# Two-layer hybrid trunk: nine instead of seven feed-forward blocks by a seven-product scheme, with its ordinary units, sums and additions placed anew

## The chip, the core and the metric

The kernel runs on one core of one Trainium2 chip. The metric is device time in microseconds (us) of one execution. In the text PE is TensorE, DVE is VectorE, ACT is ScalarE, POOL is GpSimd and SP is SyncE, which here only issues loads. A "layer" is one of the two layers of the model.

## The reference

Two layers over 256 tokens of width 2048, in float32. The first half of a layer computes `z = RMSNorm(x) @ w_in`, a gated unit on 16 channel groups, windowed attention on 16 heads, and `x += concat(RMSNorm(A), RMSNorm(B)) @ w_out`. The change bears on the second half, the feed-forward part:

```python
h2 = rms_norm(x, norm2_g[l])
x = x + (jax.nn.silu(h2 @ w_gate[l]) * (h2 @ w_up[l])) @ w_down[l]
```

`w_gate` and `w_up` are 2048 x 5632 and `w_down` is 5632 x 2048. The output is x after both layers.

## The kernel before

**Numbers in two halves.** Every weight is split into a high part `wh` (what the fast float32 form of TensorE keeps) and a rest `wl = w - wh`; activations are split likewise, once. A product is three matmuls (`mm3`, lines 124 to 127): high by high, high by low, low by high, each 128 x 128 against 128 x 512. The split of a loaded piece (`split2`, lines 89 to 98) is one cast on ACT (line 95) and one subtraction on DVE (line 96), each over 128 x 1024 elements.

**Units.** A piece is 512 KB of weights: 128 rows by two groups of 512 columns. `raw_load` (line 82) loads it from SP's queue into one of 6 rotating buffers. An ordinary unit (`unit`) loads one piece, splits it and makes 12 matmuls: two groups by two blocks of 128 tokens by three. `wh` and `wl` have 4 buffers each, so the splits can be at most four units ahead of PE. Instructions stand on each engine's queue in an order that the framework's scheduler makes at build time from the order of the program.

**The feed-forward part.** The 5632 columns of `w_gate` and `w_up` are 11 blocks of 512. An ordinary block (`gate_up`) takes 16 units, 8 for the gate and 8 for the up projection: 192 matmuls. A block by products (`seven`) sees rows of the two projections and the two token blocks as a 2 x 2 scheme and computes it by seven products instead of eight, with sums of activations (`ext`, made once in `combine`) and sums of weights: 28 product units of 6 matmuls each, 168 in all. Its first phase keeps four sums in PSUM (tiles `m`), 4 steps of four product units; each step loads three pieces (`b11`, `b12`, `b22`) and DVE makes three sums over 128 x 1024 (lines 594 to 596). The second phase keeps three (tiles `n`), 4 steps of three product units; each step loads two pieces and DVE adds one of them to a kept sum (line 621). Between and behind the phases, at a "turn", DVE and ACT combine the products out of PSUM (lines 605 to 612 and 626 to 632), and `act_T` transposes the finished block on PE and splits it.

**What stands beside the products.** The product units of the seven blocks in `S_BLOCKS` come from `s_stream`; the ordinary units, in the order of `STD_ORDER`, come from `std_stream`: the other four blocks (`gu`) and the down projection (`down`), in groups of one or two finished blocks. For each product unit 0.71 (0.5 x `STD_SHARE`) ordinary units are owed, and at a turn at least two. A `down` group whose blocks aren't finished yet yields nothing. What is left of the ordinary units runs after the last block. The down projection adds each group of output columns from PSUM to the residual `xres` on DVE (line 680). Ordinary units accumulate in the PSUM tiles `dacc`, after the last block in `acc`.

Of the kernel before, what the change touches and what calls it, by code (L numbers as in the profile page):

```python
# [12 lines left out]
F32 = mybir.dt.float32  # L13
F32R = mybir.dt.float32r
BF16 = mybir.dt.bfloat16
# [6 lines left out]
P = 128  # L22
# [4 lines left out]
HD = 64  # L27
# [12 lines left out]
NI = 3584 // NB  # L40
NFF = DFF // NB
ND = D // NB
S_BLOCKS = (1, 3, 5, 7, 8, 9, 10)
STD_ORDER = (
    ("gu", 0), ("gu", 2), ("down", (0, 1)), ("gu", 4), ("down", (2, 3)), ("gu", 6),
    ("down", (4, 5)), ("down", (6, 7)), ("down", (8, 9)), ("down", (10,)),
)
STD_SHARE = 1.42
RL = 512
WARM = 12  # L50

# [12 lines left out]
def trunk(ctx, tc, x, xt, w_in, w_out, w_gate, w_up, w_down, sgu_w, sgu_g, consts,  # L64
# [15 lines left out]
        return t.bitcast(F32)  # L80

    def raw_load(src, parts=1):
        raw = wp.tile([P, 2, NB], F32, tag="raw", name="raw", bufs=6)
        n = 2 // parts
        for i in range(parts):
            nc.sync.dma_start(raw[:, i * n : (i + 1) * n, :], src[:, i * n : (i + 1) * n, :])
        return raw
# [60 lines left out]

    cst = cp.tile([P, L, C_L], F32, tag="cst", name="cst")
    nc.sync.dma_start(cst, consts)  # L150
    junk = cp.tile([P, NB], BF16, tag="junk", name="junk")
    nc.vector.memset(junk, 1.0)
    heat = small_ps([P, NB], "heat")
    for i in range(WARM):
# [8 lines left out]
    def small(shape, name):  # L163
        return sp.tile(shape, F32, tag=name, name=name)
# [27 lines left out]
        return ps  # L192

    def sum_sq(dst, src):
        nc.scalar.activation(junk[:, : src.free_size()], src, AF.Square, accum_out=dst)

    def finish_rms(ss, width):
        tot = small([P, 1], "tot")
# [57 lines left out]
    for lay in range(L):  # L256
# [71 lines left out]
        def attend(g, t, par, zkv=zkv, kT=kT, qT=qT, ob=ob, bias=bias, layer=layer):  # L328
            nk = (t + 1) * P
            k0 = SEQ - nk  # L330
            nh = 2 * len(par)
            heads = [h for h in range(GRP) if h % 2 in par]
            step = heads[1] - heads[0]
            nkb = nk // P
            nsink = layer["nsink"]
            s = ap.tile([P, nh, nk], F32, tag="spt", name="s", bufs=4)
            for r in par:
                ps = small_ps([P, 2, nk], "ps_s")
                for i in range(2):
                    h = g * GRP + 2 * i + r  # L340
                    nc.tensor.matmul(
                        ps[:, i, :],
                        qT[h // 8][HD * r : HD * r + HD, (h % 8) // 2, t * P : (t + 1) * P],
                        kT[HD * r : HD * r + HD, g, :nk],
                        start=True,
                        stop=True,
                    )
                nc.vector.scalar_tensor_tensor(
                    s[:, par.index(r) :: len(par), :], ps, 1.0 / math.sqrt(HD),
                    bias[g][:, r::2, k0:], ALU.mult, ALU.add,  # L350
                )
            m = small([P, nh], f"m{nh}")
            nc.vector.tensor_reduce(m, s, AX.X, ALU.max)
            hs = slice(g * GRP + heads[0], (g + 1) * GRP, step)
            nm = small([P, nh], f"nm{nh}")
            nc.vector.scalar_tensor_tensor(nm, m, -1.0, nsink[:, hs], ALU.mult, ALU.min)
            es = small([P, nh], f"es{nh}")
            nc.vector.tensor_tensor(es, nm, nsink[:, hs], ALU.subtract)
            den = small([P, nh], f"den{nh}")
            for i in range(nh):  # L360
                nc.scalar.activation(
                    s[:, i, :], s[:, i, :], AF.Exp, bias=nm[:, i : i + 1],
                    accum_out=den[:, i : i + 1],
                )
            nc.scalar.activation(es, es, AF.Exp)
            rden = small([P, nh], f"rden{nh}")
            nc.vector.tensor_tensor(rden, den, es, ALU.add)
            nc.vector.reciprocal(rden, rden)
            pt = ap.tile([P, nh * nkb, P], F32, tag="spt", name="pt", bufs=4)

            def turn():
                pst = small_ps([P, nh * nkb, P], "ps_p")
                s4 = s.rearrange("p h (b k) -> p (h b) k", k=P)
                for i in range(nh * nkb):
                    nc.tensor.transpose(pst[:, i, :], s4[:, i, :], ident)
                nc.vector.tensor_copy(pt, pst)

            def weigh():
                pv = small_ps([P, nh, HD], "ps_v")
                for i in range(nh):  # L380
                    for b in range(nkb):
                        nc.tensor.matmul(  # L382
                            pv[:, i, :],
                            pt[:, i * nkb + b, :],
                            zkv[b][:, (NKV + g) * HD : (NKV + g + 1) * HD],
                            start=b == 0,
                            stop=b == nkb - 1,
                        )
                if (g, t) not in ob:
                    ob[g, t] = ap.tile([P, GRP * HD], F32, tag=f"ob{t}", name="ob", bufs=1)  # L390
                o3 = ob[g, t].rearrange("p (h d) -> p h d", d=HD)
                nc.vector.tensor_tensor(o3[:, heads[0] :: step, :], pv, bc(rden, HD), ALU.mult)

            later(3, turn)
            later(5, weigh)
# [172 lines left out]
        def seven(b, lay=lay, pairs2=pairs2, ext2=ext2, act_later=act_later):  # L568
# [9 lines left out]
            def a_op(k, t):  # L578
                return lambda p, h: pairs2[p][:, h, k, t * P : (t + 1) * P]
# [2 lines left out]
                return lambda p, h: ext2[p][:, h, n, :]  # L582

            kept = []
            for i in range(4):
                b12 = raw_load(w_up[lay, b, i, 0])
                b11 = raw_load(w_gate[lay, b, i, 0])
                b22 = raw_load(w_up[lay, b, i, 1])
                t1 = wp.tile([P, 2, NB], F32, tag="raw", name="t1", bufs=6)
                t2 = ap.tile([P, 2, NB], F32, tag="spt", name="t2", bufs=4)  # L590
                first, last = i == 0, i == 3
                s_unit(b11, 0, i, a_op(0, 0), first, last)
                yield 0.5
                nc.vector.tensor_tensor(t1, b11, b12, ALU.add)
                nc.vector.tensor_tensor(t2, t1, b22, ALU.add)
                nc.vector.tensor_tensor(b12, b12, b22, ALU.add)
                s_unit(t1, 1, i, e_op(1), first, last)
                yield 0.5
                s_unit(t2, 3, i, e_op(2), first, last)
                yield 0.5  # L600
                s_unit(b12, 2, i, e_op(0), first, last)
                yield 0.5
                kept.append(t2)
            m1 = zp.tile([P, NB], F32, tag="z", name="m1")
            nc.scalar.copy(m1, bank[0])
# [9 lines left out]
            for i in range(4):  # L615
                b21 = raw_load(w_gate[lay, b, i, 1])
                b22 = raw_load(w_up[lay, b, i, 1])
                first, last = i == 0, i == 3
                s_unit(b21, 0, i, a_op(1, 0), first, last)
                yield 0.5  # L620
                nc.vector.tensor_tensor(kept[i], kept[i], b21, ALU.add)
                s_unit(kept[i], 1, i, a_op(1, 1), first, last)
                yield 0.5
                s_unit(b22, 2, i, e_op(3), first, last)
                yield 0.5
            sg = [m1, c21]
            for t, m in ((0, m1), (1, c21)):
                nc.vector.tensor_tensor(m, bank[t], m, ALU.add)
# [36 lines left out]
        def down(blocks, final, lay=lay, pairs_f=pairs_f, norm_block=norm_block, ss1=ss1, pairs1=pairs1):  # L665
            for n in range(ND):
                while any(len(pairs_f.get(b, [])) < 2 for b in blocks):
                    yield False
                acc = new_acc() if seven_done[0] else new_acc(pd, "dacc")
                for k, b in enumerate(blocks):  # L670
                    for c in range(2):
                        pair = pairs_f[b][c]
                        unit(
                            w_down[lay, b, n, c], [(pair, 0), (pair, 1)], acc,
                            k == 0 and c == 0, k == len(blocks) - 1 and c == 1,
                        )
                        yield True
                for t in range(NTOK):
                    xs = xres[:, t, n * NB : (n + 1) * NB]
                    nc.vector.tensor_tensor(xs, acc[t], xs, ALU.add)  # L680
                    if final and lay == L - 1:
                        nc.sync.dma_start(out[t * P : (t + 1) * P, n * NB : (n + 1) * NB], xs)
                if final and lay < L - 1:
                    norm_block(n, ss1, pairs1, lay + 1, C_G1)
# [8 lines left out]
        other = std_stream()  # L693
        owed = 0.0
        for said in s_stream():
            owed = max(owed, 2.0) if said == "turn" else owed + said * STD_SHARE
            while owed >= 1.0 and next(other, False):
                owed -= 1.0
        seven_done[0] = True
        for went in other:  # L700
            if not went:
# [89 lines left out]
```

## Time and profile before

| | |
|---|---|
| median of three runs | 2026.76 us (2026.12 to 2032.09) |
| the profiled execution | 2025.57 us |
| its span, first to last instruction | 2023.9 us |
| PE busy | 1984.0 us (98%) |
| DVE busy | 1666.0 us (82%) |
| ACT busy | 1132.3 us (56%) |
| POOL busy | 67.5 us (3%) |
| moved by DMA | 416.02 MB, mean 206 GB/s |
| feed-forward part of the first layer, first product to the next layer's first matmul | 299.9 to 1015.6 us |
| of the second layer, to the last matmul | 1305.5 to 2019.3 us |

Busy time of PE is the time covered by records of matmuls, which overlap; the distance from start to start of two matmuls says what one costs. A row of the table by groups has the line, the engine, the operation, output <- inputs, shapes and the count; behind the bar busy time, mean nanoseconds of one, then the engine's idle time just before and what ended it.

### The profile page before, as it was taken

Reading aid. Unit: us, or ns where it says so; the run is one execution under the profiler, and the core shown is the slowest. Engines: PE = TensorE matmul, PEld = TensorE weight load, DVE = VectorE, ACT = ScalarE, POOL = GpSimd, SP = SyncE. Lnnn points to the kernel's source line nnn. Section 1 sums busy time; section 2 is a strip of 40 time slices with the busy share of each in tenths; the row PEclk is TensorE's granted clock in tenths of the full one; section 3 lists DMA queues with packets and bytes.
Section 4 is the critical chain, followed back from the end, with each engine's and each line's share of the span. In section 5 each row is a group of like instructions: output and inputs, shape, how many; then the busy total and the mean of one; then the engine's idle time right before and its main releaser. Section 6 shows DMA issues by size and latency. Waiting matters only on the chain.

```text
span 2023.9 us, 24694 instructions
## 1 busy us (share of the span) xinstructions
PE 1984.0 (98%) x8990; PEld 1618.5 (80%) x8990; DVE 1666.0 (82%) x1925; ACT 1132.3 (56%) x1415; POOL 67.5 (3%) x65
## 2 busy tenths in 40 slices
PE   8999999999999999999899999999999999999997
PEld 6878888888888888877687788888888888888776
DVE  5767689898989898997867776898989898989976
ACT  6455566555555555554654655666555555555543
POOL 1211000000000000000002100000000000000000
PEclk9999999999999999999999999999999999999999
DMA  9643556565766576665555344565656565657653
GB/s 323 226 162 134 187 178 227 201 235 194 238 209 234 201 236 212 234 204 193 198 188 192 131 156 179 175 233 203 239 206 234 202 239 202 233 204 241 215 186 137
DMA packets 117401, 416.02 MB, mean 206 GB/s; under 512 B 12912, under 2 KB 15088, under 8 KB 117280
## 3 DMA queue, kind: packets, MB, share of 16 engines
q1 hardware_dynamic: 115136, 407.01, 58.4%
q0 software_dynamic: 2144, 7.44, 1.2%
q8 instruction: 70, 1.15, 0.2%
q14 instruction: 51, 0.42, 0.1%
HBM read 412.27 MB, written 4.23 MB: 206 GB/s over the span
## 4 chain that ended last, share of the span: by engine, by line
PE 85%; DVE 9%; issue 2%; DMA 1%; ACT 1%; POOL 1%; SPq 0%; POOLq 0%; ACTq 0%; DVEq 0%
PE dacc L125 12%; PE dacc L126 12%; PE dacc L127 12%; PE acc L126 8%; PE acc L125 8%; PE acc L127 8%; DVE wl L96 4%; PE m L126 4%; PE m L127 4%; PE m L125 4%; PE n L126 3%; PE n L127 3%; PE n L125 3%; PE ps_v L382 1%; DMA raw<-in_w_gate_dram 1%
## 5 line engine op out<-in xcount | busy, mean ns | idle before, releaser
L95 ACT CAST wh<-raw 128x1024 fp32r<-128x1024 f32 (+1 forms) x706 | 739.5, 1050 | 593.2 <-PE dacc L127 293.2
L96 DVE TENSOR_TENSOR wl<-raw,wh 128x1024 fp32r<-128x1024 f32 (+1 forms) x706 | 853.7, 1219 | 207.9 <-ACT wh L95 198.5
L95 ACT CAST wh<-t 128x1024 fp32r<-128x1024 f32 x168 | 177.1, 1054 | 184.6 <-PE dacc L127 116.9
L125 PE MATMUL dacc<-wh,aT 128*128 128x512 f32 x640 | 251.4, 393 | 2.3 <-DVE xres L680 1.5
L127 PE MATMUL dacc<-wh,aT 128*128 128x512 f32 x640 | 250.0, 391 | 0.0
L126 PE MATMUL dacc<-wl,aT 128*128 128x512 f32 x640 | 249.9, 391 | 0.0
L96 DVE TENSOR_TENSOR wl<-t,wh 128x1024 fp32r<-128x1024 f32 x168 | 204.0, 1219 | 17.4 <-ACT wh L95 15.4
L125 PE MATMUL dacc<-wh,hT 128*128 128x512 f32 x512 | 200.3, 391 | 0.3
L126 PE MATMUL dacc<-wl,hT 128*128 128x512 f32 x512 | 199.5, 390 | 0.3 <-DVE wl L96 0.2
L127 PE MATMUL dacc<-wh,hT 128*128 128x512 f32 x512 | 199.4, 389 | 0.0
L126 PE MATMUL acc<-wl,hT 128*128 128x512 f32 x448 | 176.8, 395 | 7.8 <-DVE wl L96 7.8
L125 PE MATMUL acc<-wh,hT 128*128 128x512 f32 x448 | 180.6, 406 | 2.1 <-ACT wh L95 2.1
L127 PE MATMUL acc<-wh,hT 128*128 128x512 f32 x448 | 176.6, 394 | 0.0
L125 PEld LDWEIGHTS dacc<-wh,aT 128*128 128x128 f32 x640 | 120.1, 188 | 30.1 <-issue 3.1
L127 PEld LDWEIGHTS dacc<-wh,aT 128*128 128x128 f32 x640 | 120.7, 189 | 25.6
L126 PEld LDWEIGHTS dacc<-wl,aT 128*128 128x128 f32 x640 | 120.9, 189 | 24.5
L126 PE MATMUL m<-wl,ext 128*128 128x512 f32 x336 | 132.6, 395 | 4.6 <-DVE wl L96 4.6
L125 PE MATMUL m<-wh,ext 128*128 128x512 f32 x336 | 132.7, 395 | 1.1 <-ACT wh L95 1.1
L127 PE MATMUL m<-wh,ext 128*128 128x512 f32 x336 | 132.1, 393 | 0.0
L125 PE MATMUL acc<-wh,aT 128*128 128x512 f32 x320 | 127.8, 399 | 0.7 <-ACT aT L560 0.7
L126 PE MATMUL acc<-wl,aT 128*128 128x512 f32 x320 | 125.3, 392 | 0.0
L127 PE MATMUL acc<-wh,aT 128*128 128x512 f32 x320 | 124.1, 391 | 0.0
(157 smaller groups left out, 2980.7 us busy)
## 6 DMA issues: line engine op xcount, KB each, us to landing
raw<-in_w_up_dram SPq DMA_DIRECT2D x232, 512.0 KB, 4.3
raw<-in_w_gate_dram SPq DMA_DIRECT2D x176, 512.0 KB, 4.1
raw<-in_w_down_dram SPq DMA_DIRECT2D x176, 512.0 KB, 4.1
raw<-in_w_in_dram SPq DMA_DIRECT2D x108, 512.0 KB, 4.2
raw<-in_w_out_dram SPq DMA_DIRECT2D x64, 512.0 KB, 3.2
bias<-rdram POOLq DMA_DIRECT2D x8, 512.0 KB, 5.6
xr<-in_xt_dram SPq DMA_DIRECT2D x8, 256.0 KB, 6.0
raw<-in_w_in_dram SPq DMA_DIRECT2D x8, 256.0 KB, 5.8
```

The costliest lines, as they stand in the source:

```text
L95: nc.scalar.copy(wh[:, j : j + step, :], src)
L96: nc.vector.tensor_tensor(wl[:, j : j + step, :], src, f(wh[:, j : j + step, :]), ALU.subtract)
L125: nc.tensor.matmul(acc, ah, wh, start=first, stop=False)
L126: nc.tensor.matmul(acc, ah, wl, start=False, stop=False)
L127: nc.tensor.matmul(acc, al, wh, start=False, stop=last)
L382: nc.tensor.matmul(pv[:, i, :], pt[:, i * nkb + b, :], zkv[b][:, (NKV + g) * HD : (NKV + g + 1) * HD], start=b == 0, stop=b == nkb - 1,)
```

## The change

Seven edits, most of them in the feed-forward part.

1. Blocks 2 to 10 go by products (nine instead of seven); blocks 0 and 1 stay ordinary. The down projection's groups are ordered anew.
2. Ordinary units are owed by phase: 0.44 for each product unit of the first phase, 0.05 for each of the second, two at a turn. At most one is placed after a product unit and two at a turn.
3. The three sums of a step of the first phase are made one step ahead (`sums`).
4. The fourth sum (the kept one of the second phase) is no longer made by DVE: as soon as the third product of a step has split its sum, POOL issues a load of `w_gate` that adds onto it in SBUF.
5. The residual additions of the down projection, but those of the last group, go the same way: ACT copies PSUM to an SBUF tile, and POOL issues a DMA that adds it onto `xres`.
6. The load buffers `raw` become 7 instead of 6. Scrap outputs of `sum_sq`, the warm-up tile and the attention outputs `ob` move into the shared ring of tiles `z`.
7. Small attention tiles share one shape.

```diff
-S_BLOCKS = (1, 3, 5, 7, 8, 9, 10)
+S_BLOCKS = (2, 3, 4, 5, 6, 7, 8, 9, 10)
 STD_ORDER = (
-    ("gu", 0), ("gu", 2), ("down", (0, 1)), ("gu", 4), ("down", (2, 3)), ("gu", 6),
-    ("down", (4, 5)), ("down", (6, 7)), ("down", (8, 9)), ("down", (10,)),
+    ("gu", 0), ("down", (0, 2)), ("gu", 1), ("down", (1, 3)), ("down", (4, 5)),
+    ("down", (6, 7)), ("down", (8, 9)), ("down", (10,)),
 )
-STD_SHARE = 1.42
+SHARE_A = 0.44
+SHARE_B = 0.05
+TURN = 2
...
-        raw = wp.tile([P, 2, NB], F32, tag="raw", name="raw", bufs=6)
+        raw = wp.tile([P, 2, NB], F32, tag="raw", name="raw", bufs=7)
...
-        nc.scalar.activation(junk[:, : src.free_size()], src, AF.Square, accum_out=dst)
+        void = zp.tile([P, NB], BF16, tag="z", name="void")
+        nc.scalar.activation(void[:, : src.free_size()], src, AF.Square, accum_out=dst)
...
-                    ob[g, t] = ap.tile([P, GRP * HD], F32, tag=f"ob{t}", name="ob", bufs=1)
+                    ob[g, t] = zp.tile([P, GRP * HD], F32, tag="z", name="ob")
...
-            for i in range(4):
+            ready = {}
+
+            def sums(i):
+                b11 = raw_load(w_gate[lay, b, i, 0])
                 b12 = raw_load(w_up[lay, b, i, 0])
-                b11 = raw_load(w_gate[lay, b, i, 0])
                 b22 = raw_load(w_up[lay, b, i, 1])
-                t1 = wp.tile([P, 2, NB], F32, tag="raw", name="t1", bufs=6)
+                t1 = wp.tile([P, 2, NB], F32, tag="raw", name="t1", bufs=7)
                 t2 = ap.tile([P, 2, NB], F32, tag="spt", name="t2", bufs=4)
-                first, last = i == 0, i == 3
-                s_unit(b11, 0, i, a_op(0, 0), first, last)
-                yield 0.5
                 nc.vector.tensor_tensor(t1, b11, b12, ALU.add)
                 nc.vector.tensor_tensor(t2, t1, b22, ALU.add)
                 nc.vector.tensor_tensor(b12, b12, b22, ALU.add)
+                ready[i] = b11, t1, t2, b12
+
+            sums(0)
+            for i in range(4):
+                first, last = i == 0, i == 3
+                b11, t1, t2, t3 = ready.pop(i)
+                s_unit(b11, 0, i, a_op(0, 0), first, last)
+                yield SHARE_A
                 s_unit(t1, 1, i, e_op(1), first, last)
-                yield 0.5
+                yield SHARE_A
+                if not last:
+                    sums(i + 1)
                 s_unit(t2, 3, i, e_op(2), first, last)
-                yield 0.5
-                s_unit(b12, 2, i, e_op(0), first, last)
-                yield 0.5
+                nc.gpsimd.dma_start(t2, w_gate[lay, b, i, 1], accum_op=ALU.add)
+                yield SHARE_A
+                s_unit(t3, 2, i, e_op(0), first, last)
+                yield SHARE_A
                 kept.append(t2)
...
-                nc.vector.tensor_tensor(kept[i], kept[i], b21, ALU.add)
                 s_unit(kept[i], 1, i, a_op(1, 1), first, last)
...
-                    nc.vector.tensor_tensor(xs, acc[t], xs, ALU.add)
+                    if final:
+                        nc.vector.tensor_tensor(xs, acc[t], xs, ALU.add)
+                    else:
+                        o = zp.tile([P, NB], F32, tag="z", name="o")
+                        nc.scalar.copy(o, acc[t])
+                        nc.gpsimd.dma_start(xs, o, accum_op=ALU.add)
...
-            owed = max(owed, 2.0) if said == "turn" else owed + said * STD_SHARE
-            while owed >= 1.0 and next(other, False):
-                owed -= 1.0
+            turn = said == "turn"
+            owed += TURN if turn else said
+            for k in range(TURN):
+                if (turn or (k == 0 and owed >= 1.0)) and next(other, False):
+                    owed -= 1.0
```

More of the change, by code (lines that the diff above doesn't have):

```diff
@@ L150, in trunk @@
     nc.sync.dma_start(cst, consts)
-    junk = cp.tile([P, NB], BF16, tag="junk", name="junk")
+    junk = zp.tile([P, NB], BF16, tag="z", name="junk")
     nc.vector.memset(junk, 1.0)
@@ L351, in attend @@
                 )
-            m = small([P, nh], f"m{nh}")
+            m = small([P, GRP], "m")[:, :nh]
             nc.vector.tensor_reduce(m, s, AX.X, ALU.max)
             hs = slice(g * GRP + heads[0], (g + 1) * GRP, step)
-            nm = small([P, nh], f"nm{nh}")
+            nm = small([P, GRP], "nm")[:, :nh]
             nc.vector.scalar_tensor_tensor(nm, m, -1.0, nsink[:, hs], ALU.mult, ALU.min)
-            es = small([P, nh], f"es{nh}")
+            es = small([P, GRP], "es")[:, :nh]
             nc.vector.tensor_tensor(es, nm, nsink[:, hs], ALU.subtract)
-            den = small([P, nh], f"den{nh}")
+            den = small([P, GRP], "den")[:, :nh]
             for i in range(nh):
@@ L365, in attend @@
             nc.scalar.activation(es, es, AF.Exp)
-            rden = small([P, nh], f"rden{nh}")
+            rden = small([P, GRP], "rden")[:, :nh]
             nc.vector.tensor_tensor(rden, den, es, ALU.add)
@@ L619, in seven @@
                 s_unit(b21, 0, i, a_op(1, 0), first, last)
-                yield 0.5
-                nc.vector.tensor_tensor(kept[i], kept[i], b21, ALU.add)
+                yield SHARE_B
                 s_unit(kept[i], 1, i, a_op(1, 1), first, last)
-                yield 0.5
+                yield SHARE_B
                 s_unit(b22, 2, i, e_op(3), first, last)
-                yield 0.5
+                yield SHARE_B
             sg = [m1, c21]
```

## The prediction, made before the result was known

> **What bounds the kernel now.** I read the page's busy shares first, then the table by stretches for the two feed-forward parts (300 to 1015 us and 1305 to 2019 us), then the instructions of TensorE and VectorE in order of time inside them.
>
> ```profile
> PE 1984.0 (98%) x8990; PEld 1618.5 (80%) x8990; DVE 1666.0 (82%) x1925; ACT 1132.3 (56%) x1415; POOL 67.5 (3%) x65
> ```
>
> ```profile
> 300.00:888.00 588.00, 587.49 (x2623) 484.40 (x2622) 524.21 (x514) 339.83 (x351) 1.95 (x2) 1.00 0.65 219
> 888.00:992.00 104.00, 92.35 (x383) 71.56 (x382) 86.35 (x86) 52.02 (x55) 0.00 (x0) 0.97 0.58 201
> ...
> 1894.00:1996.00 102.00, 91.52 (x382) 71.17 (x380) 85.41 (x86) 51.73 (x55) 0.00 (x0) 0.96 0.60 205
> ```
>
> The columns are the stretch, its length, busy PE, weight loads, DVE, ACT and POOL, then granted clock, DMA share and GB/s. For 588 us of the feed-forward part PE has no gap, with DVE at 524/588 = 89%. PE idles in the last product block alone (888 to 992). So there are two things to gain: PE's own work, and that last block.
>
> PE's work goes by the spacing of matmuls, not by the 0.39 us of their records:
>
> ```profile
> 295.64 0.39 PE L127 MATMUL acc<-wh,aT 128*128 128x512 f32 x1
> ...
> 299.72 0.39 PE L127 MATMUL acc<-wh,aT 128*128 128x512 f32 x1
> ```
>
> These are 18 matmuls apart: 4.08/18 = 0.2267 us each. DVE's pace is likewise the distance of starts:
>
> ```profile
> 883.19 1.21 DVE L594 TENSOR_TENSOR t<-raw 128x1024 f32<-128x1024 f32 x1
> 884.32 1.22 DVE L96 TENSOR_TENSOR wl<-t,wh 128x1024 fp32r<-128x1024 f32 x1
> 885.46 1.21 DVE L96 TENSOR_TENSOR wl<-raw,wh 128x1024 fp32r<-128x1024 f32 x1
> 886.59 0.68 DVE L628 TENSOR_TENSOR m<-n,m 128x512 f32<-128x512 f32 x1
> 887.19 1.21 DVE L96 TENSOR_TENSOR wl<-raw,wh 128x1024 fp32r<-128x1024 f32 x1
> ...
> 890.66 0.74 DVE L632 SCALAR_TENSOR_TENSOR m<-u,nr,m 128x512 f32<-128x512 f32 x1
> 891.32 0.74 DVE L632 SCALAR_TENSOR_TENSOR c<-c,nr,c 128x512 f32<-128x512 f32 x1
> ```
>
> A 1024-wide split or sum holds DVE for 1.13 us, a 512-wide one for 0.60, one with three operands 0.66. A product unit is 6 matmuls (1.36 us of PE) and one split; an ordinary unit is 12 matmuls (2.72 us) and one split. PE is ahead of DVE only where ordinary units stand between product units. The stalls look like this:
>
> ```profile
> 900.68 0.49 PE L125 MATMUL m<-wh,ext 128*128 128x512 f32 x1 [0.86 <-ACT wh L95]
> ...
> 903.53 0.80 PE L126 MATMUL m<-wl,ext 128*128 128x512 f32 x1 [1.16 <-DVE wl L96]
> 904.13 0.63 PE L127 MATMUL m<-wh,ext 128*128 128x512 f32 x1
> 904.55 0.63 PE L125 MATMUL m<-wh,ext 128*128 128x512 f32 x1
> ...
> 986.45 0.39 PE L127 MATMUL n<-wh,ext 128*128 128x512 f32 x1
> 989.51 0.41 PE L189 MATMUL ps_f<-ident,m 128*128 128x128 f32 x2 [2.67 <-DVE m L632]
> ...
> 991.30 0.50 PE L125 MATMUL acc<-wh,aT 128*128 128x512 f32 x1 [0.35 <-ACT aT L560]
> ```
>
> After the waits matmuls start 0.42 us apart for a while, half the pace: a stall costs more than itself. At 986.45 nothing is left to run while DVE finishes the block: 4.85 us until the next weight matmul, 3.6 without that matmul's and 8 transposes' own time (0.23 and 1.0, at 0.12 each).
>
> **Calibration.** The last block's two phases, in the columns of the table by stretches:
>
> ```profile
> 888.50:964.50 76.00, 70.21 (x298) 55.54 (x297) 59.95 (x59) 35.69 (x37) 0.00 (x0) 0.98 0.59 202
> 964.50:991.30 26.80, 20.95 (x82) 15.00 (x80) 25.20 (x27) 15.86 (x18) 0.00 (x0) 0.94 0.58 199
> ```
>
> In the order of the program before I looked for five or more product units without an ordinary one between them. There are two such runs per layer, both in the last block or just ahead of it. The first has 18 units: PE 108 x 0.2267 + 1.0 for 8 transposes = 25.5 us; DVE 18 splits, 8 sums and 9 narrow operations = 35.0. Short by 9.5; the first stretch lost 9.7 (76.0 less 288 matmuls, 65.3, and 8 transposes). The second has 17 units: 23.1 against 29.8, short by 6.7; the second stretch lost 9.5 (26.8 less 72 matmuls, 16.3, and 1.0), with 3.6 of the end in it, so 5.9. The difference of sums over such a run is thus a good price.
>
> **The change, part by part.**
>
> *Two more blocks by products.* Each saves 24 matmuls (192 against 168): 2 blocks x 2 layers x 24 x 0.2267 = -21.8 us on the path. They cost 12 more splits a block: 48 x 1.13 = +54 us on DVE, 48 casts on ACT.
>
> *Sums and residual additions leave DVE.*
>
> ```profile
> L95 ACT CAST wh<-raw 128x1024 fp32r<-128x1024 f32 (+1 forms) x706 | 739.5, 1050 | 593.2 <-PE dacc L127 293.2 <-PE acc L127 157.6 <-issue 39.2
> L621 DVE TENSOR_TENSOR t<-t,raw 128x1024 f32<-128x1024 f32 x56 | 68.0, 1220 | 16.4 <-DMA raw<-in_w_gate_dram 16.4
> L680 DVE TENSOR_TENSOR xres<-dacc,xres 128x512 f32<-128x512 f32 x80 | 51.6, 681 | 0.5 <-PE dacc L127 0.3
> L605 ACT COPY m<-m 128x512 f32<-128x512 f32 x14 | 8.1, 581 | 0.5 <-PE m L127 0.5
> ```
>
> Sums go from 16 to 12 a block: 224 to 216, -9 us. The 80 residual additions go: -48 us. DVE's total stays (54 - 57 = -3) while PE's falls by 21.8, so DVE's share in the feed-forward part rises from 89% to 93%: ahead of the last sixteen ordinary units a layer has 464 wide operations (526 us) and some 107 narrow ones (66) against 2760 matmuls (626) and transposes (11). ACT gets 80 copies of 0.58 (+46) and 48 casts (+50); at 56% I cost that at nothing, its cover being the casts' idle time (593 us, mostly waiting for PE); without it each copy delays the next cast by up to 0.58, 46 at most.
>
> *Placement.* A four-product phase (16 product units) has 8 or 9 ordinary units (5 in the second block), a three-product phase mostly 1 to 4, two of them at each turn. With 8: DVE 36 x 1.13 + 5 narrow of 0.6 to 0.66 + 2 for transposed blocks = 45; PE (96 + 96) x 0.2267 + 1.0 = 44.5. With none in the three-product phase: DVE 12 x 1.13 + 4 x 0.60 = 16.0, PE 16.3. Before, that phase held 4 more sums. Runs without ordinary units in the new order, where DVE needs longer than PE, per layer: nine units across the second block's turn (9 splits, 2 sums, 4 narrow) 14.9 against 12.9; five behind them (5 splits, 2 sums) 8.0 against 6.8; eight in the fifth block (8 splits, 6 sums, 3 narrow; 8 transposes on PE) 17.7 against 11.9. Sum 9.0. DVE's lead at the start of a run may cover some (before it covered little): I take 7, plus 1 for the first block, whose first step makes two sets of sums. Gone are 15.6 of the old runs: -7.6 a layer, -15 in all. At the end two ordinary units now stand after the last block's products, and 14 behind them: of 3.6 I take 3 away, twice: -6.
>
> *Sums one step ahead.* A weight load lands in some 4.2 us (the rows of the next fence). Before, 32 loads had less DVE work than that between the release of their buffer and their first use, short by 36 us in all; DVE waited 16.4 (the row above). In the new order it is 26 loads, short by 16.4 in all, though now on a tighter engine. Bounds 0 and +16; I take +8, since four buffered units stand between DVE and PE.
>
> *Accumulating DMAs.* SP issues 8 more loads a layer (9 x 20 + 32 + 88 = 300 for 7 x 20 + 64 + 88 = 292). POOL, which issued nothing in the feed-forward part, issues 72 accumulating loads of 512 KB (one sum each) and 80 of 256 KB (residuals).
>
> ```profile
> q1 hardware_dynamic: 115136, 407.01, 58.4%
> q0 software_dynamic: 2144, 7.44, 1.2%
> raw<-in_w_up_dram SPq DMA_DIRECT2D x232, 512.0 KB, 4.3
> raw<-in_w_gate_dram SPq DMA_DIRECT2D x176, 512.0 KB, 4.1
> bias<-rdram POOLq DMA_DIRECT2D x8, 512.0 KB, 5.6
> L325 POOL DMA_DIRECT2D bias<-rdram x8 | 6.4, 804 | 4.3 <-DMA rdram<-rline 4.3
> ```
>
> An issue holds POOL 0.8 us: 152 x 0.8 = 122 us on an engine that is idle there. On POOL each waits in line for its split or its copy; a sum is used a phase later, a residual a group of output columns later, so landing at 5.6 us is early enough. No accumulating DMA is in the trace. Plain, 300 loads of 0.524 MB and 29.4 MB of accumulating in a layer of 690 us are 270 GB/s; by the first stretch (0.65 at 219) a share of 0.80. That is the lower end, cost 0; the upper end is the first rival. I take the lower, being nearer to the one row of that queue (1.2% for 7.44 MB against 58.4% for 407: a ninth more per byte). The Trainium skill says that an add in the DMA engines needs two source reads on one ring and so runs at half a copy's rate (Collectives: The Full Stack, section "The bandwidth ceiling: the fold count and why AG ≠ RS ≠ AR"). No run here shows it yet; by the row the sum below is 1991, by that rule it is the first rival's 2045.
>
> The smaller edits (seventh buffer, scrap tiles in the shared ring, shared names) I cost at 0; a ring buffer that is late would hold ACT, and PE has four units in hand there.
>
> **Sum.** 2025.57 (span 2023.9 and 1.67 around it) - 21.8 - 15 - 6 + 8 = 1991. The median of the runs is 1.2 above the profiled time, so 1991 to 1992; I say 1991. If every stall in the feed-forward part went: 2025.6 - 21.8 - 2 x 19.2 = 1965.
>
> **Rivals.**
>
> *The accumulating DMAs crowd the loads (slower).* If an add reads both of its operands through the same engines, 29.4 MB count twice: 313 GB/s, a share of 0.93 by the same row, more in four-product phases, where 4 sums and 4 to 8 residuals fall into 46 us. Loads then land later; at 6 us instead of 4.2 the slack of the new order is short by 107 us in all. If half reaches PE, +54: 2045. It decides from a landing of about 5.5 us. For it: PE waits are no longer covered by a free DVE. Against: the three-product phases have few loads and let the queue drain.
>
> *DVE becomes the pace in four-product phases.* 45 against 44.5 is a draw. If the lead isn't carried over the turn, a phase stalls by 0.5 to 1 and runs at half pace for a while (some 1.5 lost, as at 904). In half of the 18 phases: 9 x 2.3 = +21: 2012; in all, 2032. Against it: the 588 us without a gap, in which DVE also had to wait at every turn.
>
> *It does not do what it says.* The ordinary units run out again, in the second and fifth block instead of the last, with 19 us lost a layer as before and three more half-paced spells of 1.7: 2025.6 - 21.8 + 2 x 3 x 1.7 + 8 = 2022.
>
> **How the numbers follow.** Forecast 0.50 (own range 1972 to 2006), DVE's pace 0.17, crowded loads 0.25, nothing gained 0.08. A measurement of this kernel tells about 0.3% (6 us) from no change. Faster: 0.50 + 0.16 = 0.66; same: 0.01 + 0.06 = 0.07; slower: 0.25 + 0.02 = 0.27. Range 1966 to 2045: from the case without stalls, a tenth below, to the middle of the crowded case, a tenth above.
>
> **What would show it.** Right: 96 matmuls fewer; no gap of PE at the end of the last block; stalls in the fifth block of some 6 us; weight loads still landing in about 4.2 us; the software queue near 58.7/7.44 x 1.2 = 9.5% of the span. Wrong: that queue near 19%, landings of 5.5 us and more, DVE waiting for weight loads by tens of us (crowding); PE waiting for splits in most four-product phases with landings as before (DVE's pace).

## The result and the profile after

The changed kernel takes 2092.95 us (median; 2092.66 to 2094.44) against 2026.99 us for the kernel before in the same comparison: a ratio of 1.0322, 95% interval 1.0304 to 1.0339. It is 66 us slower, 102 us above the forecast of 1991 and 48 above the upper end of the range.

The page of the changed kernel (busy time by engine, DMA queues, DMA issues with their median time to landing, shares of the chain that ended last, which is followed back from the last instruction through what each step waited for):

```profile
PE 1994.1 (95%) x8894; PEld 1589.9 (76%) x8894; DVE 1678.3 (80%) x1913; ACT 1218.0 (58%) x1547; POOL 196.7 (9%) x217
...
q1 hardware_dynamic: 117440, 415.40, 56.7%
q0 software_dynamic: 24032, 66.17, 17.8%
...
PE 52%; DVE 24%; DMA 13%; issue 7%; ACT 2%; POOL 0%; SPq 0%; DVEq 0%; ACTq 0%; POOLq 0%
...
raw<-in_w_up_dram SPq DMA_DIRECT2D x248, 512.0 KB, 5.4
raw<-in_w_gate_dram SPq DMA_DIRECT2D x176, 512.0 KB, 5.1
...
t<-in_w_gate_dram POOLq DMA_DIRECT2D x72, 512.0 KB, 5.7
...
xres<-o POOLq DMA_DIRECT2D x80, 256.0 KB, 6.7
```

The 96 matmuls are gone (8990 to 8894), and DVE has as much to do as before (1678 against 1666). But the software queue takes 17.8% of the span, the loads land a microsecond later than before, and DMA stands for 13% of the chain that ended last.

Who waited for the weight loads, from the view of the line that issues them (first the kernel before, then the changed one; us in all, times):

```profile
  DVE t L621: 16.4, 23
  ACT wh L95: 14.4, 13
```

```profile
  ACT wh L97: 105.6, 47
  DVE t L596: 68.2, 40
  DVE t L597: 2.9, 4
```

The waits for loads went from 31 us to 177. The table by stretches shows where PE stood still (columns as in the prediction; the first row is the start of the first product block to the end of the eighth, layer 0; then one four-product phase, the three-product phase behind it, and the last block's three-product phase):

```profile
300.20:926.40 626.20, 588.85 (x2529) 463.94 (x2528) 536.49 (x519) 374.64 (x404) 53.79 (x62) 0.99 0.82 249
844.60:897.50 52.90, 46.94 (x201) 35.94 (x200) 43.90 (x41) 28.21 (x31) 6.93 (x8) 1.00 0.91 264
897.50:926.40 28.90, 28.05 (x121) 22.44 (x121) 24.37 (x24) 19.35 (x21) 1.74 (x2) 1.00 0.73 234
979.20:1007.30 28.10, 27.89 (x126) 22.68 (x124) 23.69 (x24) 19.64 (x22) 1.74 (x2) 1.00 0.82 265
```

The eight blocks are 2448 wide matmuls (0.2267 us each) and 80 narrow ones (0.12; one record more lies on the edge): 565 us of PE's own work in 626, so 61 us lost in one layer, where the kernel before loses 2 us by the same sum up to its last block. The four-product phase at 844.6 loses 8.4 (52.9 less 192 x 0.2267 and 8 x 0.12), the three-product phase behind it 1.7. The last block's end, which lost 9.5 before, loses half a microsecond.

What such a phase waits for, in the chain of the stretch from 853 to 884 us (start, us, what), DVE's instructions in order of time there, and the PE instruction that waits for the last of them:

```profile
854.30 1.22 DVE raw L598
855.52 2.28 DVE wl L98 x2
...
857.86 7.95 DMA raw<-in_w_up_dram
...
865.93 1.18 DVE t L596
...
869.35 1.22 DVE raw L598
870.56 3.42 DVE wl L98 x3
...
874.00 6.56 DMA raw<-in_w_down_dram
```

```profile
861.11 1.22 DVE L98 TENSOR_TENSOR wl<-raw,wh 128x1024 fp32r<-128x1024 f32 x1
865.93 1.23 DVE L596 TENSOR_TENSOR t<-raw 128x1024 f32<-128x1024 f32 x1 [3.60 <-DMA raw<-in_w_up_dram]
867.07 1.22 DVE L98 TENSOR_TENSOR wl<-t,wh 128x1024 fp32r<-128x1024 f32 x1
```

```profile
868.35 0.50 PE L128 MATMUL m<-wl,ext 128*128 128x512 f32 x1 [1.14 <-DVE wl L98]
```

It is a loop: a split frees a load buffer (857.80), the next load goes out at once (857.86), lands 7.95 us later, and the first sum of the *next* step has waited 3.60 us for it. Behind that sum, in DVE's order, stands a split of the *present* step (867.07), whose operand has long been summed and for which PE stands still until 868.35. At 870.56 it begins again.

### The profile page after: what moved, and what is told of

It is laid out like the page before. It is cut to its first block, busy times and chain, and to the rows that moved or that the text cites. A ratio compares the mean times of both kernels' runs of the same rounds, so it can differ in the third digit from the quotient of the medians.

```text
span 2091.4 us, 25132 instructions
## 1 busy us (share of the span) xinstructions
PE 1994.1 (95%) x8894; PEld 1589.9 (76%) x8894; DVE 1678.3 (80%) x1913; ACT 1218.0 (58%) x1547; POOL 196.7 (9%) x217
## 3 DMA queue, kind: packets, MB, share of 16 engines
q1 hardware_dynamic: 117440, 415.40, 56.7%
q0 software_dynamic: 24032, 66.17, 17.8%
## 4 chain that ended last, share of the span: by engine, by line
PE 52%; DVE 24%; DMA 13%; issue 7%; ACT 2%; POOL 0%; SPq 0%; DVEq 0%; ACTq 0%; POOLq 0%
DMA raw<-in_w_up_dram 12%; DVE wl L98 11%; PE acc L128 8%; PE acc L129 8%; PE acc L127 8%; PE dacc L128 4%; PE dacc L129 4%; PE dacc L127 4%; DVE raw L598 3%; DVE t L597 2%; DVE t L596 2%; PE m L128 2%; PE n L128 2%; PE n L129 2%; PE n L127 2%
## 5 line engine op out<-in xcount | busy, mean ns | idle before, releaser
L97 ACT CAST wh<-t 128x1024 fp32r<-128x1024 f32 x216 | 227.3, 1054 | 168.9 <-PE dacc L129 104.1
L98 DVE TENSOR_TENSOR wl<-t,wh 128x1024 fp32r<-128x1024 f32 x216 | 263.1, 1220 | 26.1 <-ACT wh L97 22.4
L127 PE MATMUL dacc<-wh,aT 128*128 128x512 f32 x576 | 225.0, 397 | 10.0 <-ACT wh L97 9.8
L129 PE MATMUL dacc<-wh,aT 128*128 128x512 f32 x576 | 224.9, 391 | 0.0
L128 PE MATMUL m<-wl,ext 128*128 128x512 f32 x432 | 176.5, 409 | 44.3 <-DVE wl L98 43.7
L127 PE MATMUL m<-wh,ext 128*128 128x512 f32 x432 | 171.4, 400 | 3.5 <-ACT wh L97 3.5
L129 PE MATMUL m<-wh,ext 128*128 128x512 f32 x432 | 170.4, 394 | 0.0
L612 POOL DMA_DIRECT2D t<-in_w_gate_dram x72 | 61.6, 856 | 1018.5 <-DVE wl L98 608.2
L127 PE MATMUL acc<-wh,aT 128*128 128x512 f32 x384 | 151.9, 396 | 0.0
L129 PE MATMUL acc<-wh,aT 128*128 128x512 f32 x384 | 150.0, 390 | 0.0
L596 DVE TENSOR_TENSOR t<-raw 128x1024 f32<-128x1024 f32 x72 | 88.1, 1223 | 71.5 <-DMA raw<-in_w_up_dram 68.2
L128 PEld LDWEIGHTS m<-wl,ext 128*128 128x128 f32 x432 | 81.8, 189 | 83.1 <-DVE wl L98 67.1
L127 PEld LDWEIGHTS dacc<-wh,aT 128*128 128x128 f32 x576 | 106.9, 188 | 40.8 <-ACT wh L97 16.1
L129 PEld LDWEIGHTS dacc<-wh,aT 128*128 128x128 f32 x576 | 108.3, 188 | 22.1
```

Of the source, the lines that this page charges most:

```text
L97: nc.scalar.copy(wh[:, j : j + step, :], src)
L98: nc.vector.tensor_tensor(wl[:, j : j + step, :], src, f(wh[:, j : j + step, :]), ALU.subtract)
L127: nc.tensor.matmul(acc, ah, wh, start=first, stop=False)
L128: nc.tensor.matmul(acc, ah, wl, start=False, stop=False)
L129: nc.tensor.matmul(acc, al, wh, start=False, stop=last)
L612: nc.gpsimd.dma_start(t2, w_gate[lay, b, i, 1], accum_op=ALU.add)
```

## The experiments

Each time is a median; the kernel before had 2027.2 to 2027.7 in these comparisons. Diffs are against the changed kernel unless it says otherwise. The row by stretches shown for a run is always that of the first eight product blocks of layer 0, the same 2529 or 2530 matmuls as in the 626.20 us above.

**Which of the adding DMAs.** First, each of the two went back to DVE.

```diff
-                nc.gpsimd.dma_start(t2, w_gate[lay, b, i, 1], accum_op=ALU.add)
...
+                nc.vector.tensor_tensor(kept[i], kept[i], b21, ALU.add)
```

> The changed kernel with the kept sum made by VectorE again (a 128x1024 addition in each step of the second phase); the residual additions stay accumulating DMAs. Crowding (the adding DMAs take the DMA engines twice, weight loads land late, the four-product phases stall): 37.7 of 58.7 MB of adding leave, so about two thirds of what the DMAs cost go, 2015 to 2045 us, the software queue near 7% of the span. DVE's pace (the four-product phases are too full for VectorE whatever the DMAs do): 72 more additions on VectorE, 2090 to 2120. Placement (ordinary units run out in the wrong places): within 10 us of 2093.

Measured 2071.95 us, ratio 1.0213 (1.0192 to 1.0233): inside none of the three ranges, 27 us above the one of crowding.

```diff
-                    if final:
-                        nc.vector.tensor_tensor(xs, acc[t], xs, ALU.add)
-                    else:
-                        o = zp.tile([P, NB], F32, tag="z", name="o")
-                        nc.scalar.copy(o, acc[t])
-                        nc.gpsimd.dma_start(xs, o, accum_op=ALU.add)
+                    nc.vector.tensor_tensor(xs, acc[t], xs, ALU.add)
```

> The changed kernel with the residual additions on VectorE again; the kept sum stays an accumulating DMA. Crowding: 21 of 58.7 MB leave, 2055 to 2075 us, the software queue near 12%. DVE's pace: 80 narrow additions of 0.60 us more on VectorE, 2095 to 2130. Placement: within 10 us of 2093.

Measured 2071.5 us, ratio 1.0214 (1.0188 to 1.0241), as expected for crowding. Then both edits together.

> Both sums on VectorE again: nine blocks, the placement and the sums one step ahead alone. Crowding: weight loads land in 4.1 to 4.4 us as before, the first phases lose 2 us or less each, 1985 to 2010 us, faster than the kernel before. DVE's pace: 105 us more work on VectorE, 2100 to 2150. Placement: the losses stay in the second and fifth block and at 5 us or more in all first phases, 2060 or more.

Measured 2050.32 us, ratio 1.0114 (1.0092 to 1.0135), again inside none of the ranges.

```profile
298.90:903.50 604.60, 582.10 (x2530) 464.39 (x2529) 584.82 (x579) 360.15 (x375) 1.98 (x2) 1.00 0.67 219
```

Each gives 21 us, both 43, although DVE's busy time then rises from 1678 to 1797 us. So the DMAs cost more than the DVE work that they replace, but without them the kernel is still 23 us slower than before: they are not the whole cause.

**Is it the bytes or the adding?** The same DMAs at the same places as plain copies; the kept sums then are B21 alone, and each group of down projections overwrites the residual instead of adding to it, so those additions are left out.

```diff
-                nc.gpsimd.dma_start(t2, w_gate[lay, b, i, 1], accum_op=ALU.add)
+                nc.gpsimd.dma_start(t2, w_gate[lay, b, i, 1])
...
-                        nc.gpsimd.dma_start(xs, o, accum_op=ALU.add)
+                        nc.gpsimd.dma_start(xs, o)
```

> The changed kernel with the same 152 DMAs on the same queue, waits and tiles, but copying instead of adding (the kept sum becomes the last piece alone, and the residual the last group alone: a part of both sums is left out). Crowding by the second read: the software queue at 9 to 10% of the span instead of 17.8, weight loads at 4.5 to 4.9 us, 2025 to 2060 us. If the added traffic or the work of issuing it is what costs, and not the adding: within 10 us of 2093. DVE's pace and placement: within 10 us of 2093.

Measured 2048.6 us, ratio 1.0091 (1.0068 to 1.0114). The page of this run:

```profile
q0 software_dynamic: 18912, 66.17, 9.7%
...
raw<-in_w_up_dram SPq DMA_DIRECT2D x248, 512.0 KB, 4.7
...
t<-in_w_gate_dram POOLq DMA_DIRECT2D x72, 512.0 KB, 4.3
...
xres<-o POOLq DMA_DIRECT2D x80, 256.0 KB, 4.2
```

For the same 66.17 MB the queue takes 9.7% of 2049 us as copies and 17.8% of 2091 us when they add; less the 1.2% that was there before, 174 against 347 us of the 16 engines. The adding ones take 1.3 times as long to land (5.7 to 4.3) and 1.6 times (6.7 to 4.2). In this kernel the adding alone costs 44 us. The Trainium skill says of the adds of a collective, which are made in the DMA engines, that they need two source reads and so run at half a copy's rate (Collectives: The Full Stack, section "The bandwidth ceiling: the fold count and why AG ≠ RS ≠ AR"); the trace agrees for a kernel's own adding DMAs, with a factor of 347/174 = 2.0.

**Is it the sums one step ahead?** The adding DMAs stay; loads and sums of a step go back into that step, the sums behind its first product unit as before.

```diff
             def sums(i):
...
-                nc.vector.tensor_tensor(t1, b11, b12, ALU.add)
-                nc.vector.tensor_tensor(t2, t1, b22, ALU.add)
-                nc.vector.tensor_tensor(b12, b12, b22, ALU.add)
-                ready[i] = b11, t1, t2, b12
+                ready[i] = b11, t1, t2, b12, b22
...
-            sums(0)
...
-                b11, t1, t2, t3 = ready.pop(i)
+                sums(i)
+                b11, t1, t2, t3, b22 = ready.pop(i)
                 s_unit(b11, 0, i, a_op(0, 0), first, last)
                 yield SHARE_A
+                nc.vector.tensor_tensor(t1, b11, t3, ALU.add)
+                nc.vector.tensor_tensor(t2, t1, b22, ALU.add)
+                nc.vector.tensor_tensor(t3, t3, b22, ALU.add)
...
-                if not last:
-                    sums(i + 1)
```

> The changed kernel, adding DMAs and all, with the loads and the three sums of a step made in that step again, behind its first product unit. Buffers (sums one step ahead hold three to four of the seven load buffers for a step longer, so later loads are issued too late): 2030 to 2050 us, waits for weight loads less than half of the changed kernel's 174 us. Front-loading (with the sums ahead, VectorE makes four sets of sums in the first three steps of a phase and none in the last): 2030 to 2060 us. Crowding alone (nothing but the adding DMAs is late): within 10 us of 2093.

Measured 2030.29 us (2017 to 2041 over ten runs), ratio 1.0004 (0.9979 to 1.0028). Its row by stretches, and who waited for loads:

```profile
300.20:899.30 599.10, 580.74 (x2529) 467.26 (x2528) 537.19 (x521) 372.61 (x404) 53.73 (x62) 0.99 0.85 260
```

```profile
  ACT wh L97: 57.8, 29
  DVE t L604: 7.3, 8
  DVE t L605: 6.7, 8
```

This one edit gives 63 us: DVE's waits for loads fall from 71 us to 14, ACT's from 106 to 58. The queue still takes 17.9% and loads still land in 5.1 to 6.1 us; they are now in time more often.

**Buffers held longer, or DVE's order?** In one run the loads stay one step ahead (`sums(i)` without its three additions, still called a step early), and the additions stand in their own step as in the diff above.

> The changed kernel with the loads issued, and their buffers taken, one step ahead as there, but the three sums made in their own step. Buffers: the buffers are held as long, so at most a third of what the run with both in their own step gains, 2070 to 2095 us. Front-loading: the whole of that gain, within 8 us of that run.

Measured 2063.39 us, ratio 1.0174 (1.0152 to 1.0197): 30 of the 63 us. It lies between the two expectations: the early additions are worth 30, the loads and buffers taken early the other 33, and neither part alone explains the 63. In the other run the sums stay ahead and the loads get one buffer more (for the room, the shared ring of 512-wide tiles has 6 instead of 8).

```diff
-    zp = ctx.enter_context(tc.tile_pool(name="zp", bufs=8))
+    zp = ctx.enter_context(tc.tile_pool(name="zp", bufs=6))
...
-        raw = wp.tile([P, 2, NB], F32, tag="raw", name="raw", bufs=7)
+        raw = wp.tile([P, 2, NB], F32, tag="raw", name="raw", bufs=8)
...
-                t1 = wp.tile([P, 2, NB], F32, tag="raw", name="t1", bufs=7)
+                t1 = wp.tile([P, 2, NB], F32, tag="raw", name="t1", bufs=8)
```

> The changed kernel with eight load buffers instead of seven (the shared ring of small tiles has six instead of eight to make room). Buffers: loads are issued a buffer earlier, 2050 to 2070 us. Front-loading: VectorE's work and order stay, within 10 us of 2093. The smaller ring could cost some us in the attention stage.

Measured 2046.65 us, ratio 1.0096 (1.0076 to 1.0116): one buffer gives 46 us, with the sums ahead as they were, a little more than the expected range has. So room for loads is a large part of the loss: four tiles (b11, t1, b12, b22) are taken a step earlier, and a load that gets its buffer late goes out late. The 46 can't be set against the 63 as a share of it, since an eighth buffer may help with the sums in their own step too; that wasn't run.

**Both causes apart and together.** Without the 152 DMAs, and with nothing in their place (those additions are left out), first with the sums one step ahead, then with the sums in their own step.

```diff
-                nc.gpsimd.dma_start(t2, w_gate[lay, b, i, 1], accum_op=ALU.add)
...
-                        nc.gpsimd.dma_start(xs, o, accum_op=ALU.add)
```

> The changed kernel without its 152 adding DMAs and with nothing in their place (the last piece of the kept sums and all but the last group of the residual are left out of the result): the DMA engines carry the weight loads alone, and VectorE has no more work than in the changed kernel. If the adding DMAs were all that was wrong: 1985 to 2000 us as forecast. Buffers or front-loading: 2025 to 2045 us, some 10 us under the run with plain copies in their place, with the first phases still losing 2 to 5 us each.

> The changed kernel with the sums in their own step and without its 152 adding DMAs (those additions are left out: the kept sums lack B21, and the residual gets the last group of down projections only). If late loads are the whole cause, and each of the two edits alone (2030 and 2032) removed part of it, both together give the forecast of the first text, 1985 to 2005. If what is left at 2030 is the pace of VectorE in nine product blocks, the second edit finds nothing more to gain: 2015 to 2030.

Measured 2031.61 us, ratio 1.0022 (1.001 to 1.0033), and 1995.71 us, ratio 0.9841 (0.9826 to 0.9856). The rows by stretches of the two, the second with its fifth block's and its eighth block's four-product phase:

```profile
297.60:892.00 594.40, 577.78 (x2529) 463.40 (x2528) 535.64 (x520) 374.84 (x404) 1.98 (x2) 1.00 0.68 222
```

```profile
300.20:882.30 582.10, 574.89 (x2529) 466.99 (x2528) 535.86 (x520) 373.90 (x404) 1.98 (x2) 0.99 0.70 226
588.60:643.30 54.70, 52.01 (x219) 41.34 (x217) 48.83 (x47) 29.53 (x32) 0.00 (x0) 0.94 0.68 220
808.30:853.50 45.20, 45.08 (x202) 36.47 (x200) 43.74 (x41) 27.86 (x31) 0.00 (x0) 1.00 0.77 250
```

Who waited for loads in the two, first with the sums one step ahead:

```profile
  ACT wh L97: 59.7, 42
  DVE t L596: 8.8, 17
  DVE t L597: 1.1, 4
```

```profile
  ACT wh L97: 11.5, 13
  DVE t L605: 2.2, 3
  DVE t L604: 1.6, 5
```

The four medians make a square:

| | adding DMAs | without them |
|---|---|---|
| sums one step ahead | 2093.0 | 2031.6 |
| sums in their own step | 2030.3 | 1995.7 |

Alone the DMAs cost 34.6 us and the early sums 35.9; together 97.2, so 26.7 us more than the two. Without the DMAs the early sums hardly make DVE wait for loads (10 us against 4); it is ACT's casts that wait (60 against 12). DVE's part of the loop above shows only with the late landings. One thing is not held fixed: the scheduler orders each kernel anew, and the second block's four-product phase, for one, holds 156 wide matmuls with the early sums and 178 without, so some of the 36 us may be placement. With both gone, the eighth block's four-product phase (808.3) runs as PE's own work allows (45.2 against 44.5), with DVE at 43.74 of 45.20: DVE's pace is not what stops it.

**Are the adding DMAs dear by themselves?** The kernel *before* with the two edits of e1 and e2 the other way round (56 + 80 adding DMAs), all else as it was.

> The kernel before with the two accumulating DMAs alone (kept sum and the non-final residual additions; 56 + 80 of them), its seven blocks, order, six buffers and sums in their own step kept. If doubled bytes hurt only where load buffers come free late, this costs little, and VectorE is relieved of 56 x 1.13 + 80 x 0.60 = 111 us, most of it where PE has no gap: 2015 to 2040. If the crowding by itself costs what it costs in the changed kernel (some 60 us), 2060 to 2090.

Measured 2021.53 us, ratio 0.9975 (0.9963 to 0.9987).

```profile
PE 1982.1 (98%) x8990; PEld 1617.4 (80%) x8990; DVE 1558.7 (77%) x1789; ACT 1168.6 (58%) x1495; POOL 186.0 (9%) x201
...
q0 software_dynamic: 21728, 57.78, 15.5%
```

There they cost nothing on balance: 6 us faster, with DVE relieved of 107 us. The waits for loads rose from 31 to 87 us, but on engines that had the time.

**A version that beats both.** Two more kernels: eight product blocks, sums in their own step and all on DVE, no adding DMAs; and the kernel before with one constant changed.

```diff
-S_BLOCKS = (2, 3, 4, 5, 6, 7, 8, 9, 10)
+S_BLOCKS = (1, 3, 5, 6, 7, 8, 9, 10)
 STD_ORDER = (
-    ("gu", 0), ("down", (0, 2)), ("gu", 1), ("down", (1, 3)), ("down", (4, 5)),
+    ("gu", 0), ("gu", 2), ("down", (0, 1)), ("gu", 4), ("down", (2, 3)), ("down", (4, 5)),
...
-SHARE_A = 0.44
-SHARE_B = 0.05
+SHARE_A = 0.6
+SHARE_B = 0.2
```

> Eight blocks by products, sums in their own step and all on VectorE, no adding DMAs, shares 0.6 and 0.2, seven buffers. If late loads were the cause, nothing is late here, and it gains 24 x 2 x 0.2267 = 11 us of matmuls and most of the last block's stalls (some 13 to 15 a layer of 19): 1985 to 2005. If more product blocks cost VectorE what they save PE, it is within 10 us of the kernel before: 2015 to 2035.

Measured 1985.88 us, ratio 0.9796 (0.9783 to 0.9809).

```diff
# in the kernel before
-STD_SHARE = 1.42
+STD_SHARE = 1.2
```

> The kernel before with its share of ordinary units per product step lowered from 1.42 to 1.2, so that some are left for the last block; nothing else. The 19 us a layer that PE idles in the last block go in part, and the earlier blocks have fewer ordinary units between product units. If those blocks have slack (PE has no gap there now), 1995 to 2012; if VectorE sets the pace there at once, 2020 to 2040.

Measured 1993.77 us, ratio 0.9835 (0.9821 to 0.9849), just below the lower range. The pages of the two:

```profile
PE 1967.0 (99%) x8942; PEld 1607.8 (81%) x8942; DVE 1728.2 (87%) x1995; ACT 1150.5 (58%) x1441; POOL 65.7 (3%) x65
```

```profile
q1 hardware_dynamic: 115136, 407.01, 63.1%
```

With the lower share alone, seven blocks gain 34 us: the last block's two phases, which lost 9.7 and 9.5 us in layer 0, lose 1.1 and 0.3. Over all 14 phases of both layers the stalls fall from 42 to 9 us, which is that gain. The version with eight blocks gains 8 more. Eight blocks leave DVE at 87% without any DMA's help. Nine blocks with the sums in their own step and every addition on DVE were not run, so it isn't shown which number of blocks is best.

## Why the prediction was wrong

*Matmuls, -21.8: right.* 96 fewer, at the same spacing.

*End of the last block, -6: right.* The last three-product phase loses about 0.5 us a layer (28.1 less 120 x 0.2267 and 4 x 0.12) where the forecast left 0.6.

*Starved runs, -15: too large.* The fifth block was named with "some 6" us. With both causes of the slowdown off, its four-product phase loses 7.0 in layer 0 (54.7 less 204 x 0.2267 and 12 x 0.12) and 4.5 in layer 1, so place and price hold there. But by the same sum over all 18 phases that kernel loses 18.3 us in layer 0 and 16.2 in layer 1, where the kernel before lost 21.5 and 20.6 in its 14: stalls fell by 8 us, and the two terms had 15 + 6. The forecast had 0 where the turn into a three-product phase costs 1.7 in the seventh and eighth block (16.0 of DVE against 16.3 of PE, priced as a whole, while the phase's first splits wait for a cast and stand between four narrow operations in DVE's order). It had 1 for the first block, whose four-product phase loses 1.5, and 3.2 for the two runs at the second block's turn, whose two phases lose 3.7. With the +8 left out, the forecast is 1983; measured without both causes it is 1995.7, and the stalls that did not go are the 13 us between.

*"Sums one step ahead … I take +8": the step that failed first.* It measured 36 us with the DMAs absent and 63 with them. The bound of 16 was a sum over loads of the slack between a buffer's release and its use at one landing time (4.2 us), and the reason for taking half was "since four buffered units stand between DVE and PE". But what stands on an engine runs in order: the sum on DVE that waits for a late load holds up the split behind it (865.93 above), and without the DMAs it is ACT's casts that wait (60 us against 12), so what stands between these engines and PE runs out just then. And while four tiles are held a step earlier, at most three of the seven buffers are left for loads. The seventh buffer was costed at 0; what it was worth was not run, but an eighth was worth 46 us.

*"Accumulating DMAs … That is the lower end, cost 0": wrong as well.* The nearest row of the queue was one of plain copies, and an add took the engines twice as long (347 against 174 us). Alone they cost 35 us; the upper end had 54. The first rival had the mechanism (queue near 19%, measured 17.8; DVE waiting for loads by tens of us, measured 71) but not the size, since at its 2045 it had the early sums at +8, and no term for the two together (27 us). Its threshold, "a landing of about 5.5 us", was also wrong: the medians stayed at 5.1 to 5.4, while the loads on the chain took 6.6 to 8 us; a median hides them.

*DVE's pace, the second rival: not where it was named.* The four-product phase at 808.3 loses 0.7 us at DVE 97% busy once loads are in time, and six of the nine lose 0.7 or less in layer 0. The stalls of 1.7 at the turns are of its kind, but they lie in three-product phases. The sum of DVE's wide operations is 2 us too high besides (464 x 1.13 is 524, not 526), which changes nothing.

*ACT's 80 copies, costed at 0:* the run at 1995.7 still has them, and in its eighth block's four-product phase PE loses 0.7 us. *POOL's issues, costed at 0:* the plain copies, which keep them, take 17 us more than no DMAs; how much of that is the bytes and how much the issues or the waits on them was not told apart.

## What to carry to other kernels

A step moved ahead is paid in buffers: count how many tiles it takes a step earlier, how many are left for the loads in flight, and what stands in its engine's order behind the wait. Price an accumulating DMA as two copies, and let two costs that lean on the same slack (later landings, fewer free buffers) be summed together before that slack is taken off, not each against it. And where an existing constant already sets what an elaborate edit is to bring (here the share of ordinary units), try the constant first: it gave 34 us, as much as the forecast had hoped for from the whole change.

## What the hardware showed that was not expected

A residual addition of 256 KB from one on-chip tile into another took about as long to land as an adding load of twice the bytes from DRAM: 6.7 and 5.7 us in the changed kernel, 6.9 to 7.2 and 7.2 to 8.1 in the four other kernels that have both (sums in their own step, loads ahead only, eight load buffers, and the kernel before with the DMAs). As plain copies the two took 4.2 and 4.3.

The share of a queue is not a fixed price per byte. The same 407.01 MB of the hardware queue took 58.4% of 2023.9 us in the kernel before (1182 us) and 63.1% of 1991.4 us with the lower share (1257 us), but it is not known whether on the same chip. On one chip, 415.40 MB took 62.6% (1269 us) without the adding DMAs and 58.5% (1187 us) with them and the sums in their own step. Why the time of the packets changes, the runs do not tell.
